# Turning queries and keys in square blocks and through a DRAM scratch, in a two-layer hybrid decoder

## The chip, the cores and the metric

The kernel runs on one core of a Trainium2 chip, in one launch. The metric is the device time of that launch in microseconds. Engines are named as in the profile: PE is TensorE, DVE VectorE, ACT ScalarE, POOL GpSimd, and SP the engine from whose queue nearly all DMAs are issued. L12 is line 12 of the kernel before.

## The reference

The program is a decoder trunk of two layers over 256 tokens with a width of 2048, all in fp32, each sub-layer adding into one residual stream:

```
for i in range(2):
    h = rms_norm(x, mix_norm_g[i])
    mix = fox_attention(h, ...) if i == 0 else dilated_attention(h, ...)
    x = x + mix
    h = rms_norm(x, mlp_norm_g[i])
    x = x + relu(h @ w_up)**2 @ w_down          # 2048 -> 8192 -> 2048
```

`fox_attention` is causal softmax attention of 16 heads of 128 with a bias that grows with a forget gate:

```
q, k, v, f = split(h @ w_in)
q, k = rms_norm(q per head, q_gain), rms_norm(k per head, k_gain)
c = cumsum(log_sigmoid(f + b_f))
p = softmax(causal(q @ k.T * 128**-0.5 + c_query - c_key));  out = (p @ v) @ w_out
```

`dilated_attention` has 8 value heads of width 256. For each of them there are three groups of queries and keys (128 wide, normed per head like those above), with dilations 1, 4 and 16, a causal window of 128 strided steps and a distance bias; the three groups are merged by their softmax denominators.

What matters here: every query and key head is normed over its 128 columns, multiplied by a gain per column, and has to stand with its 128 columns on the partitions before a score can be computed.

## The kernel before

**Products.** Everything large is a product of 256 tokens with 512 columns of a weight matrix, summed over 16 chunks of 128 rows (`product`, L311). An fp32 operand is cut into a rounded part and a remainder (hi and lo), and a chunk is computed by three matmuls for each of the two token tiles (L322 to L324): six matmuls per chunk. The two accumulators of a product take two of the four PSUM buffers of `ps_acc`.

**Weights.** Two chunks come in one load of 512 KB (`load`, L272, on SP's queue, five buffers; for the queries and keys of the dilated layer two DMAs of 256 KB, since a product takes 256 columns of queries and 256 of keys). `split` (L281) casts them on ScalarE (L293) and subtracts on VectorE (L294) into one of five split buffers. When a product has used a split buffer, it calls `split` for the next.

**Jobs.** All other work is written as generators (`Jobs`, L41). A product calls `jobs.tick()` after each chunk, and a job that yields a number goes on so many ticks later; one that yields a key goes on once this key is done. So the code says beside which chunk a step is written. A scheduler then orders the instructions of each engine; each engine runs its own in order.

**Queries and keys.** `qk_chain` (L445) starts at the end of each product of queries and keys: 8 in the first layer, `("fq", j)` and `("fk", j)` for the quarters j = 0 to 3, and 12 in the second, `("dqk", q4, g)` for quarter q4 and group g. It works on two tiles (t = 0, 1) of 128 tokens x 4 heads x 128 columns. ScalarE squares the accumulators into `sq` (L451), VectorE sums them, GpSimd takes the power -0.5 (L458), and three ticks later VectorE writes the normed `qn` (L464). Four ticks after that TensorE transposes the four heads of tile 0 into one PSUM buffer (L472), and a tick later those of tile 1. From PSUM ScalarE writes `whole`, the plain fp32 copy scaled by the gain (L478, for t = 0 alone), and `hi` (L486), and VectorE writes `lo` (L487). Keys need hi and lo for both tiles, queries for tile 1 alone. `sq` and `qn` live in the five buffers of tag "w".

**Heads.** `fox_head` (L631) waits for its quarter's queries and keys, for the gate and the mask, and then 2 * hh + 2 ticks, before its scores are written: a bias matmul (L639), one plain fp32 matmul for tile 0 (L546), and three matmuls with hi and lo for tile 1 (L549). `dil_head` (L681) waits for its three groups and then 4 * i + 2 ticks; the scores of its three groups are one tick apart. While the heads of a quarter are worked on, TensorE goes on with the next products.

Of the kernel before, what the change touches and what calls it, by code (L numbers as in the profile page):

```python
# [9 lines left out]
F32 = mybir.dt.float32  # L10
F32R = mybir.dt.float32r
I32 = mybir.dt.int32  # L12
AF = mybir.ActivationFunctionType
ALU = mybir.AluOpType
# [3 lines left out]
P = 128  # L18
D = 2048
S = 256  # L20
NT = S // P
# [66 lines left out]
def trunk(ctx: ExitStack, tc, x, fox_w_in, fox_b_f, fox_q_gain, fox_k_gain, fox_w_out, dil_w_in,  # L88
          dil_q_gain, dil_k_gain, dil_w_out, mix_norm_g, mlp_norm_g, mlp_w_up, mlp_w_down, out):
    nc = tc.nc  # L90
    jobs = Jobs()
# [3 lines left out]
    wpool = ctx.enter_context(tc.tile_pool(name="wpool", bufs=1))  # L95
    work = ctx.enter_context(tc.tile_pool(name="work", bufs=1))
    small = ctx.enter_context(tc.tile_pool(name="small", bufs=8))
    ps_acc = ctx.enter_context(tc.tile_pool(name="ps_acc", bufs=4, space=PSUM))
    ps_tp = ctx.enter_context(tc.tile_pool(name="ps_tp", bufs=2, space=PSUM))
    ps_sc = ctx.enter_context(tc.tile_pool(name="ps_sc", bufs=2, space=PSUM))  # L100
# [5 lines left out]
    ident = const.tile([P, P], F32, name="ident")  # L106
# [14 lines left out]
    gain = const.tile([P, 4 * KC + 8], F32, name="gain")  # L121
# [111 lines left out]
    for q4 in range(4):  # L233
        for g in range(3):
            c = g * DH * P + q4 * 2 * P
# [67 lines left out]
    def by_column(acc, apart=NC // 2):  # L303
        return acc.rearrange("p (b n h) -> p b h n", n=apart, h=2)

    def halves(t, apart=NC // 2):
        return t.rearrange("p (b h n) -> p b h n", n=apart, h=2)
# [134 lines left out]
        return lambda k: (tag, k // 2)  # L442


    def qk_chain(acc, tag, key, parts):  # L445

        yield (tag, "rstd")
        sq = []
        for t in range(NT):
            s = work.tile([P, NC], F32, tag="w", name=f"sq_{key}_{t}", bufs=5)  # L450
            nc.scalar.activation(halves(s), by_column(acc[t]), AF.Square, scale=rstd[tag][:, t:t + 1])  # L451
            sq.append(s)
        ss = small.tile([P, NT, 4], F32, tag="ss", name=f"ss_{key}")
        for t in range(NT):
            nc.vector.tensor_reduce(ss[:, t, :], sq[t].rearrange("p (h d) -> p h d", h=4), AX.X, ALU.add)
        nc.vector.tensor_scalar(ss, ss, 1.0 / P, EPS, ALU.mult, ALU.add)
        rq = small.tile([P, NT, 4], F32, tag="rq", name=f"rq_{key}")
        nc.gpsimd.tensor_tensor(rq, ss, mhalf.rearrange("p (t h) -> p t h", t=NT), ALU.pow)  # L458
        yield 3
        qn = []  # L460
        for t in range(NT):
            nc.vector.tensor_scalar_mul(rq[:, t, :], rq[:, t, :], rstd[tag][:, t:t + 1])
            q = work.tile([P, 4, P], F32, tag="w", name=f"qn_{key}_{t}", bufs=5)
            nc.vector.tensor_mul(q.rearrange("p (h g) d -> p h g d", h=2),  # L464
                                 acc[t].rearrange("p (g d h) -> p h g d", h=2, g=2),
                                 rq[:, t, :].rearrange("p (h g) -> p h g", h=2).unsqueeze(3).to_broadcast([P, 2, 2, P]))
            qn.append(q)
        yield 4
        for t in range(NT):
            pt = ps_tp.tile([P, 4, P], F32, tag="tp", name=f"ptq_{key}_{t}")  # L470
            for h in range(4):
                nc.tensor.transpose(pt[:, h, :], qn[t][:, h, :], ident)  # L472
            for c, nh, gcol, (whole, hi, lo) in parts:
                src = pt[:, c // P:c // P + nh, :]
                gc = gain[:, gcol:gcol + 1]
                keys = hi.shape[2] == S
                if t == 0:
                    nc.scalar.activation(whole, src, AF.Copy, scale=gc)  # L478
                    if not keys:
                        continue  # L480
                at = slice(t * P, (t + 1) * P) if keys else slice(0, P)
                for i in range(nh):

                    order = [x.rearrange("p (h n) -> p h n", h=2) for x in (hi[:, i, at], lo[:, i, at])]
                    of = src[:, i, :].rearrange("p (n h) -> p h n" if keys else "p (h n) -> p h n", h=2)
                    nc.scalar.activation(order[0], of, AF.Copy, scale=gc)  # L486
                    nc.vector.scalar_tensor_tensor(order[1], of, gc, order[0].bitcast(F32), ALU.mult, ALU.subtract)  # L487
            yield 1
        jobs.done.add(key)

    def v_chain(acc, tag, key, dst):
# [228 lines left out]
    def dilated(tag):  # L720
        for q4 in range(4):
            qTs = [heads_pair(f"dqT{q4}_{g}", g, False) for g in range(3)]
            kTs = [heads_pair(f"dkT{q4}_{g}", 3 + g, True) for g in range(3)]
            for g in range(3):
                product(keys_h(tag), lhs_h(tag),
                        lambda acc: qk_chain(acc, tag, ("dqk", q4, g),
                                             [(0, 2, DIL_G + g, qTs[g]), (2 * P, 2, DIL_G + 3 + g, kTs[g])]))
            vt = values(f"dv{q4}")
            for i in range(2):
                jobs.spawn(dil_head(q4, i, qTs, kTs, vt))  # L730
            product(keys_h(tag), lhs_h(tag), lambda acc: v_chain(acc, tag, ("dv", q4), vt))
# [114 lines left out]
    tag = "n0"  # L846
    for j in range(4):
        sel = make_sel(j)
        qT = [heads_pair(f"fqT{j}_{i}", i, False) for i in range(2)]
        kT = [heads_pair(f"fkT{j}_{i}", 3 + i, True) for i in range(2)]  # L850
        vt = values(f"fv{j}")
        product(keys_h(tag), lhs_h(tag), lambda acc: qk_chain(
            acc, tag, ("fq", j), [(0, 2, FOX_G, qT[0]), (2 * P, 2, FOX_G, qT[1])]))
        if j == 0:
            jobs.need("wf")
            gate(tag)
        product(keys_h(tag), lhs_h(tag), lambda acc: qk_chain(
            acc, tag, ("fk", j), [(0, 2, FOX_G + 1, kT[0]), (2 * P, 2, FOX_G + 1, kT[1])]))

        for hh in range(4):  # L860
            jobs.spawn(fox_head(j, hh, qT, kT, vt, sel))
        product(keys_h(tag), lhs_h(tag), lambda acc: v_chain(acc, tag, ("fv", j), vt))
# [42 lines left out]
```

## Time and profile before

| | |
|---|---|
| time, median of 3 runs | 2186.88 us (2186.87 to 2187.01) |
| profiled execution | 2186.94 us |
| its span, first to last instruction | 2185.1 us |
| granted clock | 1.0 |
| TensorE matmul busy | 2175.9 us (100%) |
| VectorE, ScalarE, GpSimd busy | 1372.8, 1099.9, 49.3 us |
| moved by DMA | 425.78 MB, 195 GB/s |

All busy times and starts come from the one profiled execution. Matmuls are pipelined: the duration shown for one (0.38 us for 512 columns) is longer than the time by which it moves the next, which is read from the starts of neighbours. A line "A <- B: total, times, longest" in the list of waits says that A sat idle until B was done.

### The profile page before, as it was taken

Reading aid. Unit: us, or ns where it says so; the run is one execution under the profiler, and the core shown is the slowest. Engines: PE = TensorE matmul, PEld = TensorE weight load, DVE = VectorE, ACT = ScalarE, POOL = GpSimd, SP = SyncE. Lnnn points to the kernel's source line nnn. Section 1 sums busy time; section 2 is a strip of 40 time slices with the busy share of each in tenths; the row PEclk is TensorE's granted clock in tenths of the full one; section 3 lists DMA queues with packets and bytes.
Section 4 is the critical chain, followed back from the end, with each engine's and each line's share of the span. In section 5 each row is a group of like instructions: output and inputs, shape, how many; then the busy total and the mean of one; then the engine's idle time right before and its main releaser. Section 6 shows DMA issues by size and latency. Waiting matters only on the chain.

```text
span 2185.1 us, 29948 instructions
## 1 busy us (share of the span) xinstructions
PE 2175.9 (100%) x11464; PEld 1937.9 (89%) x11464; DVE 1372.8 (63%) x1810; ACT 1099.9 (50%) x1517; POOL 49.3 (2%) x52
## 2 busy tenths in 40 slices
PE   9999999999999999999999999999999999999999
PEld 7888888998998998998888888888988988988988
DVE  6776685655665565566666767665655655655564
ACT  6565555544454454454555555555544544544442
POOL 1011000000000000000000000000000000000000
PEclk9999999999999999999999999999999999999999
DMA  7566555656666666665555565656656656656664
GB/s 246 171 183 186 175 175 198 196 203 203 201 202 204 202 201 203 202 201 198 195 186 176 182 193 168 198 178 191 201 203 202 201 203 202 201 203 204 201 212 144
DMA packets 248832, 425.78 MB, mean 195 GB/s; under 512 B 16824, under 2 KB 66544, under 8 KB 248688
## 3 DMA queue, kind: packets, MB, share of 16 engines
q1 hardware_dynamic: 248096, 423.19, 60.4%
q8 instruction: 90, 1.47, 0.3%
q10 hardware_dynamic: 560, 0.66, 0.1%
q14 instruction: 54, 0.44, 0.1%
q0 software_dynamic: 32, 0.02, 0.0%
HBM read 421.70 MB, written 2.10 MB: 194 GB/s over the span
## 4 chain that ended last, share of the span: by engine, by line
PE 98%; DVE 1%; ACT 0%; issue 0%; DMA 0%; POOL 0%; ACTq 0%; POOLq 0%
PE acc L322 21%; PE acc L324 21%; PE acc L323 21%; PE up_n3a_acc L370 5%; PE up_n1a_acc L370 5%; PE up_n3a_tp L370 3%; PE up_n3a_sc L370 3%; PE up_n1a_sc L370 3%; PE up_n1a_tp L370 3%; PE up_n1a_acc L374 3%; PE up_n3a_acc L374 3%; PE up_n1a_tp L374 1%; PE up_n1a_sc L374 1%; PE up_n3a_sc L374 1%; PE up_n3a_tp L374 1%; PE ptx_n L406 1%
## 5 line engine op out<-in xcount | busy, mean ns | idle before, releaser
L294 DVE TENSOR_TENSOR wl<-raw,wh 128x1024 fp32r<-128x1024 f32 (+1 forms) x801 | 978.7, 1223 | 703.8 <-ACT wh L293 697.0
L293 ACT CAST wh<-raw 128x1024 fp32r<-128x1024 f32 (+1 forms) x801 | 838.4, 1047 | 881.9 <-PE acc L324 525.8
L322 PE MATMUL acc<-wh,hT_n 128*128 128x512 f32 x896 | 346.0, 387 | 0.2 <-ACT wh L293 0.2
L323 PE MATMUL acc<-wl,hT_n 128*128 128x512 f32 x896 | 340.3, 380 | 0.1
L324 PE MATMUL acc<-wh,hT_n 128*128 128x512 f32 x896 | 340.2, 380 | 0.0
L322 PE MATMUL acc<-wh,aTh_n1a 128*128 128x512 f32 x512 | 194.5, 380 | 0.0
L323 PE MATMUL acc<-wl,aTh_n1a 128*128 128x512 f32 x512 | 194.0, 379 | 0.0
L324 PE MATMUL acc<-wh,aTl_n1a 128*128 128x512 f32 x512 | 194.0, 379 | 0.0
L324 PEld LDWEIGHTS acc<-wh,hT_n 128*128 128x128 f32 x896 | 169.7, 189 | 23.9
L322 PEld LDWEIGHTS acc<-wh,hT_n 128*128 128x128 f32 x896 | 169.6, 190 | 21.9 <-ACT wh L293 0.6
L323 PEld LDWEIGHTS acc<-wl,hT_n 128*128 128x128 f32 x896 | 170.0, 190 | 21.3 <-DVE wl L294 0.4
L322 PE MATMUL acc<-wh,aTh_n3a 128*128 128x512 f32 x480 | 181.9, 379 | 0.0
L323 PE MATMUL acc<-wl,aTh_n3a 128*128 128x512 f32 x480 | 181.9, 379 | 0.0
L324 PE MATMUL acc<-wh,aTl_n3a 128*128 128x512 f32 x480 | 181.9, 379 | 0.0
L370 PE MATMUL up_n3a_acc<-hT_n,wh 128*128 128x512 f32 x512 | 181.6, 382 | 0.0
L370 PE MATMUL up_n1a_acc<-hT_n,wh 128*128 128x512 f32 x512 | 181.6, 382 | 0.0
L374 PE MATMUL up_n1a_acc<-hT_n,wl 128*128 128x256 f32 x512 | 139.6, 273 | 0.0
L374 PE MATMUL up_n3a_acc<-hT_n,wl 128*128 128x256 f32 x512 | 139.6, 273 | 0.0
L324 PEld LDWEIGHTS acc<-wh,aTl_n1a 128*128 128x128 f32 x512 | 96.8, 189 | 13.7
L323 PEld LDWEIGHTS acc<-wl,aTh_n1a 128*128 128x128 f32 x512 | 96.8, 189 | 13.6
L370 PEld LDWEIGHTS up_n1a_acc<-hT_n,wh 128*128 128x128 f32 x512 | 96.8, 189 | 13.5
L322 PEld LDWEIGHTS acc<-wh,aTh_n1a 128*128 128x128 f32 x512 | 96.8, 189 | 13.5
(732 smaller groups left out, 3207.1 us busy)
## 6 DMA issues: line engine op xcount, KB each, us to landing
raw<-in_mlp_w_up_dram SPq DMA_DIRECT2D x256, 512.0 KB, 4.2
raw<-in_mlp_w_down_dram SPq DMA_DIRECT2D x256, 512.0 KB, 3.8
raw<-in_dil_w_in_dram SPq DMA_DIRECT2D x192, 256.0 KB, 2.9
raw<-in_fox_w_in_dram SPq DMA_DIRECT2D x95, 512.0 KB, 3.9
raw<-in_fox_w_out_dram SPq DMA_DIRECT2D x32, 512.0 KB, 3.6
raw<-in_dil_w_in_dram SPq DMA_DIRECT2D x32, 512.0 KB, 3.7
raw<-in_dil_w_out_dram SPq DMA_DIRECT2D x32, 512.0 KB, 3.6
out_dram<-x SPq DMA_DIRECT2D x7, 256.0 KB, 5.9
```

Source lines behind the costliest of these rows:

```text
L293: issued["cast"] = nc.scalar.copy(hi[:, part, :], raw[:, part, :])
L294: nc.vector.tensor_sub(lo[:, part, :], raw[:, part, :], hi[:, part, :].bitcast(F32))
L322: nc.tensor.matmul(acc[t], ah[:, tok], hi, start=first, stop=False)
L323: nc.tensor.matmul(acc[t], ah[:, tok], lo, start=False, stop=False)
L324: issued["product"] = nc.tensor.matmul(acc[t], al[:, tok], hi, start=False, stop=last)
L370: issued["product"] = nc.tensor.matmul(banks[b], hi[:, i, col], in_turn(tokens.rearrange("p x s -> p (x s)"), P // 2), start=first, stop=last)
L374: nc.tensor.matmul(banks[b][:, 0:S], lo[:, i, col], in_turn(tokens[:, 0, :], P // 2), start=False, stop=False)
L406: issued["transposed"] = nc.tensor.transpose(pt[:, i, t * P:(t + 1) * P], xt[n][:, t, c:c + P], ident)
```

## The change

In 18 of the 20 chains, all but `("fk", 3)` and `("dqk", 3, 2)`, the transposition is done in two other ways together. VectorE transposes each 32 x 32 block of `qn` in place of the whole (`nc.vector.transpose`, into the buffer of `sq`). The blocks are then moved to their places by DMAs: for each tile, four stores of 64 KB, one per 32 partitions, from `sq` into a DRAM scratch, and one reload of 256 KB from it into `qn`. All of these are issued from SP's queue. The rest of the chain is written 8 + 1 + 1 ticks after `qn`, where it was 4 + 1 + 1, and reads SBUF instead of PSUM: ScalarE scales two heads at once, into `whole` or, for the second tile, into `sq[0]`, and copies that into `hi`, and VectorE subtracts for `lo`.

```diff
+    dram = ctx.enter_context(tc.tile_pool(name="dram", bufs=1, space=bass.MemoryType.DRAM))
...
+    by_engine = {("fk", 3), ("dqk", 3, 2)}
+
     def qk_chain(acc, tag, key, parts):
...
             qn.append(q)
-        yield 4
-        for t in range(NT):
-            pt = ps_tp.tile([P, 4, P], F32, tag="tp", name=f"ptq_{key}_{t}")
-            for h in range(4):
-                nc.tensor.transpose(pt[:, h, :], qn[t][:, h, :], ident)
-            for c, nh, gcol, (whole, hi, lo) in parts:
...
+        if key in by_engine:
+            yield 4
...
+            jobs.done.add(key)
+            return
+
+
+        for t in range(NT):
+            turned = sq[t].rearrange("p (j h r) -> p j h r", j=4, h=4)
+            nc.vector.transpose(turned.rearrange("p j h r -> p h j r"),
+                                qn[t].rearrange("p h (j c) -> p h j c", c=32))
+            blocks = dram.tile([4, 32, 4, P], F32, tag="blocks", name=f"blocks_{key}_{t}", bufs=4)
+            for i in range(4):
+                nc.sync.dma_start(blocks[:, :, i, :].rearrange("j c x -> c j x"), sq[t][32 * i:32 * i + 32].rearrange("p (j x) -> p j x", j=4))
+            nc.sync.dma_start(qn[t], blocks.rearrange("j c i x -> (j c) (i x)").rearrange("p (h d) -> p h d", h=4))
+        yield 8
+        for t in range(NT):
+            yield 1
+            for n, (c, nh, gcol, (whole, hi, lo)) in enumerate(parts):
                 keys = hi.shape[2] == S
...
+                src = qn[t].rearrange("p i (h r) -> p h i r", h=4)[:, c // P:c // P + nh]
+                to = sq[0].rearrange("p (n i x) -> p n i x", n=2, i=2)[:, n] if t else whole
+                nc.scalar.activation(to.rearrange("p h (i r) -> p h i r", i=4), src, AF.Copy, scale=gain[:, gcol:gcol + 1])
+                if t == 0 and not keys:
+                    continue
                 at = slice(t * P, (t + 1) * P) if keys else slice(0, P)
...
+                a, b = (x[:, :, at].rearrange("p i (h n) -> p i h n", h=2) for x in (hi, lo))
+                of = to.rearrange("p i (n h) -> p i h n" if keys else "p i (h n) -> p i h n", h=2)
+                nc.scalar.copy(a, of)
+                nc.vector.tensor_sub(b, of, a.bitcast(F32))
         jobs.done.add(key)
```

More of the change, by code (lines that the diff above doesn't have):

```diff
@@ L467, in qk_chain @@
             qn.append(q)
-        yield 4
-        for t in range(NT):
-            pt = ps_tp.tile([P, 4, P], F32, tag="tp", name=f"ptq_{key}_{t}")
-            for h in range(4):
-                nc.tensor.transpose(pt[:, h, :], qn[t][:, h, :], ident)
-            for c, nh, gcol, (whole, hi, lo) in parts:
-                src = pt[:, c // P:c // P + nh, :]
-                gc = gain[:, gcol:gcol + 1]
-                keys = hi.shape[2] == S
[L477 to L480, printed above, removed]
-                at = slice(t * P, (t + 1) * P) if keys else slice(0, P)
[L482 to L488, printed above, removed]
+        if key in by_engine:
+            yield 4
+            for t in range(NT):
+                pt = ps_tp.tile([P, 4, P], F32, tag="tp", name=f"ptq_{key}_{t}")
+                for h in range(4):
+                    nc.tensor.transpose(pt[:, h, :], qn[t][:, h, :], ident)
+                for c, nh, gcol, (whole, hi, lo) in parts:
+                    src = pt[:, c // P:c // P + nh, :]
+                    gc = gain[:, gcol:gcol + 1]
+                    keys = hi.shape[2] == S
+                    if t == 0:
+                        nc.scalar.activation(whole, src, AF.Copy, scale=gc)
+                        if not keys:
+                            continue
+                    at = slice(t * P, (t + 1) * P) if keys else slice(0, P)
+                    for i in range(nh):
+                        order = [x.rearrange("p (h n) -> p h n", h=2) for x in (hi[:, i, at], lo[:, i, at])]
+                        of = src[:, i, :].rearrange("p (n h) -> p h n" if keys else "p (h n) -> p h n", h=2)
+                        nc.scalar.activation(order[0], of, AF.Copy, scale=gc)
+                        nc.vector.scalar_tensor_tensor(order[1], of, gc, order[0].bitcast(F32), ALU.mult, ALU.subtract)
+                yield 1
+            jobs.done.add(key)
+            return
@@ new lines, in qk_chain @@
+        yield 8
+        for t in range(NT):
+            yield 1
+            for n, (c, nh, gcol, (whole, hi, lo)) in enumerate(parts):
+                keys = hi.shape[2] == S
+                src = qn[t].rearrange("p i (h r) -> p h i r", h=4)[:, c // P:c // P + nh]
+                to = sq[0].rearrange("p (n i x) -> p n i x", n=2, i=2)[:, n] if t else whole
+                nc.scalar.activation(to.rearrange("p h (i r) -> p h i r", i=4), src, AF.Copy, scale=gain[:, gcol:gcol + 1])
+                if t == 0 and not keys:
+                    continue
+                at = slice(t * P, (t + 1) * P) if keys else slice(0, P)
+                a, b = (x[:, :, at].rearrange("p i (h n) -> p i h n", h=2) for x in (hi, lo))
+                of = to.rearrange("p i (n h) -> p i h n" if keys else "p i (h n) -> p i h n", h=2)
+                nc.scalar.copy(a, of)
+                nc.vector.tensor_sub(b, of, a.bitcast(F32))
```

## The prediction

> **What bounds the kernel now.** I read the page first (span, busy times, the chain that ended last), then who waited for whom, then TensorE's timeline around one product of queries and keys.
>
> ```profile
> span 2185.1 us, 29948 instructions
> ...
> PE 2175.9 (100%) x11464; PEld 1937.9 (89%) x11464; DVE 1372.8 (63%) x1810; ACT 1099.9 (50%) x1517; POOL 49.3 (2%) x52
> ...
> PEclk9999999999999999999999999999999999999999
> ...
> q1 hardware_dynamic: 248096, 423.19, 60.4%
> ...
> PE 98%; DVE 1%; ACT 0%; issue 0%; DMA 0%; POOL 0%; ACTq 0%; POOLq 0%
> ```
>
> 98% of the chain lies on TensorE, at the full granted clock. A busy PE need not be a PE at its peak, so the waits decide. TensorE's own list is this short:
>
> ```profile
> PE spare L116 <- POOL ident masks.py:199: 2.5, 1, 2.5
> PE ps_g_mix L135 <- DMA g_mix<-in_mix_norm_g_dram: 1.9, 1, 1.9
> PE sc_d L546 <- DVE sd L693: 0.8, 4, 0.2
> PE pc L610 <- DVE g_lf L607: 0.2, 1, 0.2
> PE acc L322 <- ACT wh L293: 0.2, 1, 0.2
> ```
>
> After the start it waits 1.2 us in all. Everybody else waits for TensorE:
>
> ```profile
> DVE wl L294 <- ACT wh L293: 697.0, 592, 1.8
> ACT wh L293 <- PE acc L324: 525.8, 375, 2.0
> ...
> ACT wh L293 <- DMA raw<-in_fox_w_in_dram: 4.6, 5, 3.1
> ```
>
> ```profile
> SPq L272 <- DVE wl L294: 1310.3, 620, 4.4
> ```
>
> ScalarE's weight casts wait until TensorE releases a split buffer, VectorE's subtractions wait for the casts, and SP's loads wait for the subtractions; the reverse, a cast waiting for its load, happened five times. So an instruction taken from TensorE is worth the time by which it moves the next product, as long as nothing new makes TensorE wait.
>
> **What is removed: 144 transposes.** Of 20 chains, 18 lose 2 tiles x 4 transposes: 36 groups of four. Their price is read from the starts of the products around them (second key product, the timeline of PE):
>
> ```profile
> 139.83 0.38 PE L322 MATMUL acc<-wh,hT_n 128*128 128x512 f32 x1
> ...
> 141.55 0.38 PE L324 MATMUL acc<-wh,hT_n 128*128 128x512 f32 x1
> 141.77 0.60 PE L472 MATMUL ptq_('fk', 1)_0_1504<-ident,qn_('fk', 1)_0_1463 128*128 128x128 f32 x4
> 142.13 0.46 PE L322 MATMUL acc<-wh,hT_n 128*128 128x512 f32 x1
> 142.43 0.38 PE L323 MATMUL acc<-wl,hT_n 128*128 128x512 f32 x1
> ...
> 147.83 0.33 PE L639 MATMUL sc_f<-negc,sel 128*128 128x384 f32 x1
> 147.99 0.38 PE L546 MATMUL sc_f<-fkT_0w,fqT_0w 128*128 128x128 f32 x2
> 148.13 0.36 PE L549 MATMUL sc_f<-fkT_0h,fqT_0h 128*128 128x256 f32 x1
> 148.32 0.28 PE L549 MATMUL sc_f<-fkT_0l,fqT_0h 128*128 128x256 f32 x1
> ```
>
> From 139.83 to 141.55 lie eight steps, so a product advances TensorE by 0.215 us, and a step of the jobs (six products) by 1.29 us. From the L324 at 141.55 to the L323 at 142.43 pass 0.88 us where two steps would be 0.43: a group costs 0.45 us. 36 x 0.45 = 16.2 us. Nothing on TensorE takes their place.
>
> The Trainium skill ("TensorE: Matmul & The Clock Gate", Part 4: PE-mode transpose) gives about 275 ns for one transpose inside a kernel. By that figure as a cost, 144 of them would be worth an estimated 39.6 us. The starts above do not bear it out as a cost: 0.45 us per four is 0.11 us each.
>
> **What is added on VectorE and ScalarE.** The written order of the changed kernel has both block transposes right behind the second qn. No row shows such a transpose. The bounds are other 128x512 operations: 0.42 us (the cast to sel) and 0.74 us (a subtraction from PSUM, L496); I take 0.68, the qn product.
>
> ```profile
> 140.04 0.68 DVE L464 TENSOR_TENSOR qn_('fk', 1)_1_1466<-acc,rq_('fk', 1)_1434 128x512 f32<-128x512 f32 x1
> 140.64 2.35 DVE L294 TENSOR_TENSOR wl<-raw,wh 128x1024 fp32r<-128x1024 f32 x2
> ...
> 157.65 0.74 DVE L496 SCALAR_TENSOR_TENSOR fv1l<-acc,rstd_n,fv1h 128x512 fp32r<-128x512 f32 x1
> ...
> 159.44 0.42 DVE L677 CAST sel<-self 128x512 fp32r<-128x512 f32 x1
> ```
>
> Two per chain, 36 in all: 24 us of VectorE, which is idle 37% of the span; the following weight subtraction comes 1.4 us later. The subtractions and copies behind the transposition become fewer and wider, about as much work as before. Priced at nothing: the cover is that a weight split is made four buffers ahead of its use, 4 x 2 x 1.29 = 10.3 us.
>
> ```profile
> 135.54 1.05 ACT L293 CAST wh<-raw 128x1024 fp32r<-128x1024 f32 x1 [0.95 <-ACT sq_('fk', 1)_1_1428 L451]
> 138.13 1.05 ACT L293 CAST wh<-raw 128x1024 fp32r<-128x1024 f32 x1 [1.53 <-PE acc L324]
> ...
> 142.41 0.47 ACT L478 ACTIVATE fkT_0w<-ptq_('fk', 1)_0_1504,gain 128x256 f32<-128x256 f32 x1 [0.68 <-PE ptq_('fk', 1)_0_1504 L472]
> ```
>
> ```profile
> L515 DVE TENSOR_TENSOR oTfl<-po_f,oTfh 128x256 fp32r<-128x256 f32 x16 | 6.6, 416 | 0.0
> ```
>
> Casts come every 2.59 us and end 1.05 us later, the subtraction some 1.2 us after that (half of 2.35 above): about 8 us of the 10.3 remain.
>
> **What is added on SP: ten DMAs per chain, and waits in its queue.** Eight stores of 64 KB, two reloads of 256 KB. The order on SP is: four stores of the first tile, three of the second, reload 0 (waits until the four have landed), the eighth store, two weight loads, reload 1 (waits for its four stores). The weight loads behind them wait with them.
>
> ```profile
> raw<-in_dil_w_in_dram SPq DMA_DIRECT2D x192, 256.0 KB, 2.9
> ...
> out_dram<-x SPq DMA_DIRECT2D x7, 256.0 KB, 5.9
> ...
> out_dram<-x ACTq DMA_DIRECT2D x1, 128.0 KB, 1.9
> ```
>
> ```profile
> L765 SPq DMA_DIRECT2D out_dram<-x x6: 356/357/366, 2119.6 to 2161.7; - x6
> ```
>
> The next line is that of L272, the weight loads, between 130 and 152 us:
>
> ```profile
> DMA to landing us min/median/max: 3.9/4.5/5.5
> ```
>
> An issue takes 0.36 us. A store lands after 1.9 us at best (128 KB, nothing beside it) and 5.9 at worst (256 KB beside loads); I take 1.9, since 64 KB is nearer to the first, and keep the other for a rival. A reload lands after 2.9 (256 KB) to 4.5 us (the 512 KB loads in this window).
>
> On the second key product: qn ends at 140.72, the transposes at 141.4 and 142.1; the fourth store leaves at 142.5 and lands at 144.4; reload 0 goes out then, the eighth store at 144.8, landing at 146.7; reload 1 goes out then and lands between 149.6 and 151.2. SP is held some 5.7 us, two loads in between. Its cover: a load is issued when its buffer is free, five weight steps (12.9 us) ahead of its cast; less 2.3 for cast and subtraction and 5.5 for the slowest landing, 5.1 us remain, and then the 8 us above. Queue share: 0.5 MB written and 0.5 MB read per chain and 20.7 us (16 job steps), 18 MB on 423, beside a queue at 60.4%: priced at nothing.
>
> **Who waits for the result.** The chain now ends 8 + 1 + 1 steps after qn instead of 4 + 1 + 1, so the scores of its heads stand four steps later. 147.83 was step 11; without the two groups step 15 is 141.77 + 8 x 1.29 = 152.1. The written order puts three more products behind the first score, so L549, which needs both tiles, comes at 153.05 and the one with fkT_0l at 153.45. ScalarE reaches the second tile's scaling only after the seventh weight cast behind the squares, which TensorE's pace allows at 135.54 + 6 x 2.59 = 151.1; so it starts at 152.1, and reload 1 (151.2 at the latest by the rows) is there. A scaling takes 0.47 (L478 above), a copy of 128x256 takes
>
> ```profile
> L514 ACT CAST oTfh<-po_f 128x256 fp32r<-128x256 f32 x16 | 5.9, 368 | 6.4 <-PE po_f L513 6.4
> ```
>
> 0.37, the subtraction 0.42 (L515). Two scalings and a copy make fkT_0h ready at 153.4, and the subtraction fkT_0l at 153.85: 0.4 us late. I take 0.5. This is met at the first head of the first three quarters of the forgetting attention: 1.5 us. In the dilated layer the scores of the last group come two steps (2.6 us) later, so the first three quarters there wait for nothing by these rows; I add 1.5 us for landings that vary. The later heads, and the two products left on TensorE, wait as before.
>
> **The sum.** The profiled execution took 2186.94 us, 1.84 more than its span, and agrees with the median of 2186.88. 2186.94 - 16.2 + 3 = 2173.7, so 2174. With no stall it is 2170.7.
>
> **Rivals.**
> Half eaten: the four stores of a tile (256 KB) together land like the 256 KB store, 5.9 us after the first: reload 0 at 147.3, the eighth store, alone, issued at 147.7, lands at 149.6 (after 1.9) to 151.6 (after 3.9, half way to 5.9), reload 1 at 152.5 to 156.1. ScalarE then waits 0.4 to 4.0 us. With the 0.5 us from above, three forgetting heads at up to 4.5 and three dilated at up to 1.9 make up to 19 us, in the middle some 10: 2186.94 - 16.2 + 10 = 2181. For it: that row stands beside weight loads, as these stores will. Against it: these are a quarter of its size.
>
> Slower: every store lands like that row. Reload 0 goes out at 148.4, the eighth store lands at 154.7, reload 1 at 159.2, 7.1 us after ScalarE wants it: 7.6 x 3 + 5.0 x 3 = 38 us, less 16.2 is +22: 2209. It decides from 4.7 us per forgetting head (3 x 4.7 + 3 x 2.1 = 20.4), a round trip some 5 us above mine. SP's hold would then pass 13 us and use up the loads' cover too.
> The Trainium skill ("DMA: Bandwidth & Descriptors", Rules for kernel authors) speaks for this side: it warns against transposing by a plain DMA with a rearranged access pattern, 19 times slower than the hardware's. No run here shows such a DMA, and this one moves runs of 512 bytes, the elements inside the blocks being turned by VectorE.
>
> More than the sum: each transpose is worth its whole shown duration (0.27 us): 2186.94 - 39 = 2148. The starts above speak against it. That the change does less than it says is excluded by the order: 144 transposes are gone from TensorE's.
>
> **How the numbers follow.** Forecast, 2170 to 2179: 0.71. Half eaten, 2179 to 2188: 0.15, half of it below 2182.5. Slower: 0.12. More gain: 0.02. What can be told from no change is 0.2%, 4.4 us. So faster 0.80 (0.71 + 0.07 + 0.02), same 0.08, slower 0.12. The range 2170 to 2184 holds the forecast and over half of the second case.
>
> **What would show it.** Right: TensorE's busy time some 16 us lower, ordinary 0.215 us steps where the groups stood, a total of a few us of PE waits at L549 or its counterpart in three to six places, block transposes near 0.7 us, stores landing in about 2 us and ScalarE's scaling of the second tile hardly waiting for its DMA. Wrong: stores landing in 4 us or more, PE waits of 3 us and more at the first scores of each quarter, or weight casts waiting for raw loads around the chains.

## The result and the profile after

| | before | after |
|---|---|---|
| time, median | 2186.88 us (2186.06 to 2187.01, 6 runs) | 2201.18 us (2196.70 to 2209.25, 6 runs) |
| profiled execution | 2186.94 us | 2206.46 us |
| its span | 2185.1 us | 2204.7 us |
| mean granted clock | 1.0 | 0.995 |

The changed kernel is slower: ratio 1.0073, 95% interval 1.0061 to 1.0084. The forecast was 2174, within 2170 to 2184. The kernel before repeats within 1 us, the changed one within 12.6, and its shortest run (2196.70 us) has the highest mean clock (0.998), its longest (2209.25 us) the lowest (0.994). The page of the changed kernel (lines of the changed file: L323 to L325 are the products, L579 and L582 the scores):

```profile
span 2204.7 us, 29840 instructions
PE 2171.6 (98%) x11320; PEld 1932.2 (88%) x11320; DVE 1382.7 (63%) x1793; ACT 1101.0 (50%) x1500; POOL 48.5 (2%) x52
PE 81%; DMA 7%; DVE 4%; issue 3%; SPq 2%; ACT 2%; POOL 1%; ACTq 0%; DVEq 0%; POOLq 0%
```

The 144 transposes are gone, but TensorE's busy time fell by only 4.3 us (2175.9 to 2171.6) where 16.2 were forecast, and its idle time, span less busy, rose from 9.2 to 33.1 us. The chain that ended last lies on TensorE for 81%, where it was 98%. Who TensorE waits for, in the changed kernel (total, times, longest):

```profile
PE sc_d L579 <- DVE sd L726: 10.8, 5, 4.1
PE sc_f L582 <- ACT fkT_0h L520: 10.2, 3, 3.9
PE tq_('dqk', 3, 2)_0_12793 L477 <- DVE qn_('dqk', 3, 2)_0_12752 L468: 2.8, 1, 2.8
```

Nearly all of this lies at the first heads of the first three quarters of both layers; the last line is one of the two chains whose transposes stayed on TensorE. On the second key product, the timeline of TensorE:

```profile
155.19 0.33 PE L672 MATMUL sc_f<-negc,sel 128*128 128x384 f32 x1
...
156.01 0.38 PE L325 MATMUL acc<-wh,hT_n 128*128 128x512 f32 x1
160.29 0.58 PE L582 MATMUL sc_f<-fkT_0h,fqT_0h 128*128 128x256 f32 x1 [3.90 <-ACT fkT_0h L520]
...
161.51 0.63 PE L324 MATMUL acc<-wl,hT_n 128*128 128x512 f32 x1
161.94 0.63 PE L325 MATMUL acc<-wh,hT_n 128*128 128x512 f32 x1
...
163.18 0.38 PE L325 MATMUL acc<-wh,hT_n 128*128 128x512 f32 x1
163.40 0.38 PE L323 MATMUL acc<-wh,hT_n 128*128 128x512 f32 x1
```

The score comes 3.9 us late, and then, until 163.18, a product advances TensorE by 0.43 us instead of 0.215. By 10 us windows (the length, then TensorE's, weight loads', VectorE's, ScalarE's and GpSimd's busy time, the granted clock, the share of the DMA engines, and GB/s):

```profile
150.00:160.00 10.00, 6.39 (x31) 5.30 (x29) 5.28 (x6) 4.73 (x9) 0.00 (x0) 0.99 0.85 269
160.00:170.00 10.00, 9.71 (x47) 8.67 (x48) 8.33 (x23) 6.21 (x17) 0.00 (x0) 0.84 0.54 177
```

Before, the clock was 1.00 in both windows. So a late score is paid twice: by its wait, and by a lower clock behind it. ScalarE's timeline shows where the wait comes from:

```profile
131.27 0.51 ACT L513 ACTIVATE fqT_0w<-qn_('fq', 1)_0_1283,gain 128x256 f32<-128x256 f32 x1 [2.03 <-DMA qn_('fq', 1)_0_1283<-blocks_('fq', 1)_0_1289]
...
136.51 0.91 ACT L513 ACTIVATE sq_('fq', 1)_0_1246<-qn_('fq', 1)_1_1286,gain 128x256 f32<-128x256 f32 x2 [1.12 <-DMA qn_('fq', 1)_1_1286<-blocks_('fq', 1)_1_1296]
...
137.92 0.68 ACT L455 ACTIVATE sq_('fk', 1)_0_1430<-acc,rstd_n 128x512 f32<-128x512 f32 x1
...
148.92 1.05 ACT L294 CAST wh<-raw 128x1024 fp32r<-128x1024 f32 x1 [1.54 <-PE acc L325]
153.46 0.51 ACT L513 ACTIVATE fkT_0w<-qn_('fk', 1)_0_1467,gain 128x256 f32<-128x256 f32 x1 [3.49 <-DMA qn_('fk', 1)_0_1467<-blocks_('fk', 1)_0_1473]
...
159.02 0.91 ACT L513 ACTIVATE sq_('fk', 1)_0_1430<-qn_('fk', 1)_1_1470,gain 128x256 f32<-128x256 f32 x2 [0.89 <-DMA qn_('fk', 1)_1_1470<-blocks_('fk', 1)_1_1480]
159.84 0.40 ACT L520 CAST fkT_0h<-sq_('fk', 1)_0_1430 128x256 fp32r<-128x256 f32 x1
```

ScalarE runs in order. It waits for a reload at 131.27, 136.51, 153.46 and 159.02, and everything behind these scalings waits too: weight casts and, at 137.92, the squares of the next chain. SP's queue and the block transposes between them:

```profile
145.58 0.68 DVE L468 TENSOR_TENSOR qn_('fk', 1)_1_1470<-acc,rq_('fk', 1)_1438 128x512 f32<-128x512 f32 x1
146.18 0.70 DVE L500 STREAM_TRANSPOSE sq_('fk', 1)_0_1430<-qn_('fk', 1)_0_1467 128x512 f32<-128x512 f32 x1
146.81 0.67 DVE L500 STREAM_TRANSPOSE sq_('fk', 1)_1_1432<-qn_('fk', 1)_1_1470 128x512 f32<-128x512 f32 x1
```

```profile
146.91 1.79 SPq L504 DMA_DIRECT2D blocks_('fk', 1)_0_1473<-sq_('fk', 1)_0_1430  x4
148.80 1.37 SPq L504 DMA_DIRECT2D blocks_('fk', 1)_1_1480<-sq_('fk', 1)_1_1432  x3
150.47 0.34 SPq L505 DMA_DIRECT2D qn_('fk', 1)_0_1467<-blocks_('fk', 1)_0_1473  x1
150.86 0.43 SPq L504 DMA_DIRECT2D blocks_('fk', 1)_1_1480<-sq_('fk', 1)_1_1432  x1
151.34 0.97 SPq L273 DMA_DIRECT2D raw<-in_fox_w_in_dram  x2
153.72 0.34 SPq L505 DMA_DIRECT2D qn_('fk', 1)_1_1470<-blocks_('fk', 1)_1_1480  x1
```

The order is the one forecast. The first block transpose ends at 146.88, reload 1 goes out at 153.72 and has landed at 159.02, 12.1 us after the transpose. Over the whole kernel, ScalarE's waits for reloads add up to 65.2 us in its list of waits. Over all chains, the issues of the stores (first line) and of the reloads (second):

```profile
DMA to landing us min/median/max: 1.7/2.1/3.8
```

```profile
DMA to landing us min/median/max: 2.7/4.6/6.0
```

In the dilated layer the wait takes one more turn. VectorE, then ScalarE, then TensorE:

```profile
1251.07 0.43 DVE L521 TENSOR_TENSOR dqT_2l<-sq_('dqk', 1, 2)_0_10980,dqT_2h 128x256 fp32r<-128x256 f32 x1 [1.01 <-ACT dqT_2h L520]
1251.42 0.42 DVE L521 TENSOR_TENSOR dkT_2l<-sq_('dqk', 1, 2)_0_10980,dkT_2h 128x256 fp32r<-128x256 f32 x1
1251.75 0.55 DVE L726 SCALAR_TENSOR_TENSOR sd<-dist,sc_d 128x384 f32<-128x384 f32 x1
```

```profile
1249.84 0.91 ACT L513 ACTIVATE sq_('dqk', 1, 2)_0_10980<-qn_('dqk', 1, 2)_1_11023,gain 128x256 f32<-128x256 f32 x2 [1.03 <-DMA qn_('dqk', 1, 2)_1_11023<-ks_('dqk', 1, 2)_1_11033]
```

```profile
1252.44 0.77 PE L579 MATMUL sc_d<-dkT_2w,dqT_2w 128*128 128x128 f32 x2 [4.14 <-DVE sd L726]
```

The third score of the head needs one of the two PSUM buffers that the first two hold. The bias step that frees it (L726) stands in VectorE's queue behind the subtractions of the last group, which wait for ScalarE's copies and so for the reload.

### The profile page after: what moved, and what is told of

Same layout as the page of the kernel before. It is cut to its first block, busy times and chain, and to the rows that moved or that the text cites. A ratio compares the mean times of both kernels' runs of the same rounds, so it can differ in the third digit from the quotient of the medians.

```text
span 2204.7 us, 29840 instructions
## 1 busy us (share of the span) xinstructions
PE 2171.6 (98%) x11320; PEld 1932.2 (88%) x11320; DVE 1382.7 (63%) x1793; ACT 1101.0 (50%) x1500; POOL 48.5 (2%) x52
## 4 chain that ended last, share of the span: by engine, by line
PE 81%; DMA 7%; DVE 4%; issue 3%; SPq 2%; ACT 2%; POOL 1%; ACTq 0%; DVEq 0%; POOLq 0%
PE acc L323 16%; PE acc L324 16%; PE acc L325 16%; PE up_n3a_acc L371 5%; PE up_n1a_acc L371 5%; PE up_n3a_sc L371 3%; PE up_n3a_tp L371 3%; PE up_n1a_sc L371 3%; PE up_n1a_tp L371 3%; PE up_n1a_acc L375 3%; PE up_n3a_acc L375 3%; DVE wl L295 2%; DMA raw<-in_dil_w_in_dram 2%; SPq L504 1%; PE up_n1a_tp L375 1%
## 5 line engine op out<-in xcount | busy, mean ns | idle before, releaser
L323 PE MATMUL acc<-wh,hT_n 128*128 128x512 f32 x896 | 347.0, 388 | 0.0
L325 PE MATMUL acc<-wh,hT_n 128*128 128x512 f32 x896 | 342.7, 383 | 0.0
L323 PE MATMUL acc<-wh,aTh_n1a 128*128 128x512 f32 x512 | 194.5, 380 | 0.0
L325 PE MATMUL acc<-wh,aTl_n1a 128*128 128x512 f32 x512 | 194.0, 379 | 0.0
L325 PEld LDWEIGHTS acc<-wh,hT_n 128*128 128x128 f32 x896 | 171.4, 191 | 24.8
L323 PEld LDWEIGHTS acc<-wh,hT_n 128*128 128x128 f32 x896 | 171.8, 192 | 22.9 <-ACT hT_n L412 0.3
L323 PE MATMUL acc<-wh,aTh_n3a 128*128 128x512 f32 x480 | 181.9, 379 | 0.0
L325 PE MATMUL acc<-wh,aTl_n3a 128*128 128x512 f32 x480 | 181.9, 379 | 0.0
L325 PEld LDWEIGHTS acc<-wh,aTl_n1a 128*128 128x128 f32 x512 | 96.8, 189 | 13.7
L323 PEld LDWEIGHTS acc<-wh,aTh_n1a 128*128 128x128 f32 x512 | 96.8, 189 | 13.5
```

Source lines behind the costliest of these rows:

```text
L323: nc.tensor.matmul(acc[t], ah[:, tok], hi, start=first, stop=False)
L325: issued["product"] = nc.tensor.matmul(acc[t], al[:, tok], hi, start=False, stop=last)
```

## The experiments

Theory A, formed from these rows: the loss is the wait for the reloads, spread by the in-order queues of ScalarE and VectorE, and the clock behind each wait. Rival B: the held SP queue and the traffic delay the weights.

**What the transposes are worth: double_transposes.** The kernel before, each group of four done twice.

```diff
-            for h in range(4):
-                nc.tensor.transpose(pt[:, h, :], qn[t][:, h, :], ident)
+            for _ in range(2):
+                for h in range(4):
+                    nc.tensor.transpose(pt[:, h, :], qn[t][:, h, :], ident)
```

> The kernel before, with each group of four transposes on TensorE done twice into the same place: 40 groups more. By the price read from the starts of the products (0.45 us a group) 2186.9 + 18 = 2205 us (2203 to 2207). If transposes are hidden (theory C): 2187 to 2189. If each cost its shown duration of 0.27 us: 2230.

2204.73 us, ratio 1.0083 (1.0066 to 1.0099): 17.85 us over the 2186.88 of before for 40 groups, 0.446 each. The first term of the sum holds.

**The change without its round trip: no_round_trip.** The stores and reloads are left out, so the scores are computed from blocks that stay where VectorE left them.

```diff
...
-            for i in range(4):
-                nc.sync.dma_start(blocks[:, :, i, :]..., sq[t][32 * i:32 * i + 32]...)
-            nc.sync.dma_start(qn[t], blocks...)
...
-                src = qn[t]...
-                to = sq[0]...
+                src = sq[t]...
+                to = qn[0]...
```

> The stores and reloads are left out: VectorE transposes the blocks, and the blocks are then read where they lie, so the scores are computed from queries and keys whose blocks were not moved. All other instructions and the later steps stay. A and B alike: 2186.9 - 16.2 = 2170 to 2173 us, no waits at the scores, full clock. C, or VectorE's block transposes as the cause: 2187 or more.

2172.02 us (2171.79 to 2172.28), ratio 0.9933 (0.9918 to 0.9948).

```profile
PE 2159.6 (100%) x11320; PEld 1924.7 (89%) x11320; DVE 1384.4 (64%) x1793; ACT 1103.1 (51%) x1500; POOL 48.7 (2%) x52
```

TensorE's busy time is 16.3 us below that of before, and the block transposes, the wider copies and the later heads cost it next to nothing. So the round trips cost the changed kernel 2201.2 - 2172.0 = 29 us. In the profiled execution (2204.7 - 2170.1 = 34.6 us of span) 12.0 us of that are TensorE busy for longer with the same matmuls, and 22.6 are idle.

**The round trip made, but not waited for: unread_round_trip and unread_apart.** Both issue every DMA, and compute the scores from the unmoved blocks. First with both reloads into `qn[1]`, then with every DMA's buffers as in the change:

```diff
-            nc.sync.dma_start(qn[t], blocks...)
+            nc.sync.dma_start(qn[1], blocks...)     # unread_round_trip alone
...
-                src = qn[t]...
+                src = sq[t]...                      # both; to = qn[0] in the first
```

> The changed kernel with all its stores and reloads still issued at their places, both reloads of a chain into qn[1], which nobody reads: as in no_round_trip the scalings read the blocks where VectorE left them, so the scores are of unmoved blocks. Traffic and SP's queue are then those of the changed kernel; only the wait for the result is gone. Theory A (the loss is the wait for the reload, through ScalarE's in-order queue, and the clock behind it): 2172 to 2176, within 0.2% of no_round_trip's 2172.0. Rival B (the held SP queue and 18 MB of traffic delay the weights, and that costs TensorE time by itself): 2180 to 2200; each us above 2172 is B's share of the changed kernel's 29.

2185.38 us, ratio 0.9995 (0.9986 to 1.0005), which looks like 13 us for B. But the first reload overwrites what the second block transpose still has to read:

```profile
DVE sq_('fk', 1)_1_1432 L500 <- DMA qn_('fk', 1)_1_1470<-blocks_('fk', 1)_0_1473: 4.5, 1, 4.5
```

VectorE waited there as ScalarE does in the change, so this kernel separates nothing.

> As unread_round_trip, but every store and reload keeps the buffer it has in the changed kernel; only the scalings read the blocks in sq[t] in place of qn[t]. In unread_round_trip the first reload went into qn[1], which VectorE's second block transpose still had to read, so VectorE waited 4 to 4.5 us for a reload in several chains, and its 2185.4 is no measure of traffic alone. Here nobody waits for a reload except whoever takes its buffer next. Theory A (the loss is the wait for the result, with ScalarE's queue and the clock behind it): 2172 to 2176. Rival B (held SP queue and traffic): 2180 to 2190; each us above 2172.0 is B's share of the changed kernel's 29.

2174.49 us (2172.02 to 2175.45), ratio 0.9942 (0.9927 to 0.9956). All stores and reloads are issued and land. The held queue and the traffic do delay the weights (ScalarE waits 25.9 us in all for loads, against 5.5 in no_round_trip), but TensorE hardly notices: they cost about 2.5 us, the wait for the result and what follows from it about 27.

**Later scores: late_scores.** The heads of the first three quarters four ticks (5.2 us) later.

```diff
-        yield 2 * hh + 2
+        yield 2 * hh + 2 + (4 if j < 3 else 0)
...
-        yield 4 * i + 2
+        yield 4 * i + 2 + (4 if q4 < 3 else 0)
```

> The chains and their DMAs stay as in the changed kernel; the heads of the first three quarters of each attention layer write their scores four job steps (5.2 us) later. Theory A (the loss is TensorE waiting at the first scores of a quarter for the second reload, and the lower clock behind these waits): the waits of 3 to 4 us are covered, the 16 us of the transposes are left as gain, 2169 to 2176 us. Theory B (the DMAs of the round trip hold up the weight loads all along): the time hardly changes, 2195 to 2205. Theory C (the transposes on TensorE cost nothing, so there was nothing to gain): not below 2187.

2189.0 us (2183.73 to 2194.56), ratio 1.0009 (0.9999 to 1.0018). 12 us come back: more than B expected, and less than A in this first form, in which the waits at the first scores were the whole loss. The forgetting layer's scores no longer wait for `fkT_0h`, but ScalarE is still held (57.3 us of waits for reloads) and others are late (`sc_d` 6.7 us, `ptp_f` 3.3). More time ahead of the score alone is no remedy.

**Fewer chains by DMA: early_chains and urgent_chains.** The chains whose scores come first stay on TensorE (24 groups of four go), or they alone go by DMA (12 groups go).

```diff
-    by_engine = {("fk", 3), ("dqk", 3, 2)}
+    by_engine = {("fk", j) for j in range(4)} | {("dqk", j, 2) for j in range(4)}     # early_chains
+    by_engine = {("fq", j) for j in range(4)} | {("dqk", j, g) for j in range(4) for g in range(2)} | {("fk", 3), ("dqk", 3, 2)}     # urgent_chains
```

> Only the 12 chains whose result is needed a product or more later (the queries of the first layer, groups 0 and 1 of the second) go through blocks and DMAs; all keys of the first layer and group 2 of the second stay on TensorE. A: 24 groups of four transposes at 0.45 us are 10.8 us of gain and nobody waits at the scores: 2175 to 2180 us. B: 12 of the 18 round trips, so about two thirds of the loss stay, 2193 to 2200. C: not below 2187.

2186.45 us (2182.74 to 2188.63), ratio 0.9998 (0.9989 to 1.0008): 9 us above the 2177.4 that it would be without loss (2172.0 of no_round_trip and 12 groups more on TensorE, 5.4), which neither theory had expected. No product of the remaining 12 chains is wanted soon, yet TensorE waits, for the next chain's `qn`:

```profile
PE tq_('dqk', 3, 2)_0_12799 L477 <- DVE qn_('dqk', 3, 2)_0_12758 L468: 1.9, 1, 1.9
...
PE tq_('dqk', 2, 2)_0_11933 L477 <- DVE qn_('dqk', 2, 2)_0_11892 L468: 1.5, 1, 1.5
```

By these rows it is ScalarE's queue at work (42.1 us of waits for reloads): a chain with time to spare holds ScalarE and so delays one that has none. early_later, below, puts this to the test.

> The opposite of early_chains: only the six chains that the next scores wait for (keys of quarters 0 to 2, group 2 of quarters 0 to 2) go through blocks and DMAs. Gain 12 groups x 0.45 = 5.4 us. A with the waits as they were: 2187 - 5.4 + 30 = 2211. A2 (part of each wait comes from the chain before, whose round trip held ScalarE): the waits are about 2.5 us shorter each, 2188 to 2198 us. B: one third of the traffic, 2185 to 2192.

2196.77 us, ratio 1.0043 (1.0028 to 1.0058). Without loss it would be 2182.8 (2172.0 and 24 groups more), so six chains by themselves lose 14 us. With the 9 us that the other twelve lose by themselves this makes 23 of the 29; neither by itself accounts for the rest. Their forgetting scores wait 6.3 us in all against 10.2 in the change, which fits A: here no query chain holds ScalarE ahead of the key chain's squares, and what is left is the chain's own round trip.

**ScalarE's queue left free: later_scalings.** Three more ticks between `qn` and the scalings (the heads follow three ticks later too), and the scalings placed behind the weight cast written last.

```diff
-        yield 8
+        yield 11
...
+                with behind(issued["cast"]):
                     nc.scalar.activation(to..., src, AF.Copy, scale=gain[:, gcol:gcol + 1])
```

> As the changed kernel, but the steps behind the round trip are written 11 + 1 + 1 job steps after qn, not 8 + 1 + 1, and each scaling is kept behind the newest weight cast on ScalarE, so that two more casts (5.2 us) stand before the first scaling; the heads follow three steps later. Theory A2 (what is left of the loss once the scores are late is ScalarE's queue: it waits in order for a reload, and the weight casts and the next chain's squares behind it come late): ScalarE hardly waits for a DMA, 2172 to 2178 us. Theory A alone (only the waits at the first scores): as late_scores, about 2187. Theory B (the DMAs beside the weight loads): 2185 or more.

2182.8 us (2179.78 to 2187.72), ratio 0.9984 (0.9975 to 0.9993): 18 of the 29 us come back with every DMA as before, less than A2 expected. ScalarE's waits for reloads fall to 6.0 us. How much of the 18 is the freed queue and how much the later heads, these runs do not tell apart; late_scores, with heads four ticks later and ScalarE still held, gave 12. On the second key product ScalarE, and TensorE's wait behind it:

```profile
153.17 1.04 ACT L294 CAST wh<-raw 128x1024 fp32r<-128x1024 f32 x1 [2.59 <-DMA raw<-in_fox_w_in_dram]
154.12 0.50 ACT L514 ACTIVATE fkT_0w<-qn_('fk', 1)_0_1467,gain 128x256 f32<-128x256 f32 x1
```

```profile
158.55 0.38 PE L583 MATMUL sc_f<-fkT_0h,fqT_0h 128*128 128x256 f32 x1 [0.91 <-ACT fkT_0h L521]
```

ScalarE no longer waits for the reload, but for a weight load; such waits add up to 34.9 us here, against 12.7 in the change. From 153.17 it is busy without a gap until it casts `fkT_0h` at 158.08, and TensorE waits 0.91 us for that cast. So here some of what is left of the loss came by way of a late weight load.

**Two ways around SP's queue: reload_first and pool_queue.** Loads written after a chain are issued behind its latest reload; or stores and reloads are issued by GpSimd.

```diff
-                with hold(t[:, 0, 0:1]):
+                with hold(t[:, 0, 0:1]), behind(*([issued["reload"]] if "reload" in issued else [])):
...
-            nc.sync.dma_start(qn[t], blocks...)
+            issued["reload"] = nc.sync.dma_start(qn[t], blocks...)     # reload_first
...
-                nc.sync.dma_start(...)
+                nc.gpsimd.dma_start(...)                               # pool_queue, all ten
```

> As the changed kernel, but a weight load written after a reload is also issued after it, so the second reload no longer stands behind two weight loads on SP and in the DMA queues. A and A2: the second reload lands some 2 us earlier and each of the waits at the first scores shrinks by about as much: 2186 to 2194 us. B: the weight loads now wait longer, so 2201 or more.

2306.41 us, ratio 1.0547 (1.0531 to 1.0563), far from every expectation.

```profile
144.83 1.65 SPq L273 DMA_DIRECT2D raw<-in_fox_w_in_dram  x2
159.00 1.79 SPq L504 DMA_DIRECT2D blocks_('fk', 1)_0_1473<-sq_('fk', 1)_0_1430  x4
```

The edit held back not two loads but every load written after a chain: nothing left SP for 12.5 us, the weights ran out (TensorE waits 26.0 us for casts), and with them the squares came late. It says nothing on A or B, and shows what it costs to stop the loads behind a chain.

> As the changed kernel, with the stores and reloads issued from GpSimd's queue, so that SP issues weight loads alone and never waits for a store. B in the form that SP is held: the loss goes, 2171 to 2180 us. A and A2: the round trip is as long or longer, 2195 to 2210 us, with the same waits at the first scores.

2287.73 us, ratio 1.0463 (1.0445 to 1.048), outside both expectations.

```profile
157.36 2.22 POOL L504 DMA_DIRECT2D blocks_('fk', 1)_0_1473<-sq_('fk', 1)_0_1430  x4 [1.28 <-DVE sq_('fk', 1)_0_1430 L500]
...
164.32 0.57 POOL L505 DMA_DIRECT2D qn_('fk', 1)_0_1467<-blocks_('fk', 1)_0_1473  x1 [3.12 <-DMA blocks_('fk', 1)_0_1473<-sq_('fk', 1)_0_1430]
...
169.62 0.56 POOL L505 DMA_DIRECT2D qn_('fk', 1)_1_1470<-blocks_('fk', 1)_1_1480  x1 [4.18 <-DMA blocks_('fk', 1)_1_1480<-sq_('fk', 1)_1_1432]
```

SP is free, and the kernel is 87 us slower than with SP held: reload 1 goes out 12.3 us after the first store began, against 6.8 on SP, since the stores landed after 4.2 us in the median instead of 2.1. The page counts these DMAs under another kind of queue (software_dynamic, 18.90 MB) than SP's (hardware_dynamic). On this product ScalarE then waits 12.4 us for reload 0. So a free SP does not bring the loss back, and a longer round trip makes it larger; GpSimd, which now waits for the stores, also has a step of every chain in its queue, and what that adds was not measured.

**The clock by itself: early_transposes.** The kernel before, without any DMA more: in the six chains whose scores come first, `qn` and TensorE's transposes are written earlier, the heads where they were.

```diff
+        early = key in [("fk", 0), ("fk", 1), ("fk", 2), ("dqk", 0, 2), ("dqk", 1, 2), ("dqk", 2, 2)]
-        yield 3
+        yield 0 if early else 3
...
-        yield 4
+        yield 0 if early else 4
...
+        if early:
+            yield 7
         jobs.done.add(key)
```

> The kernel before, with no DMA added: in six chains (keys of the first three quarters, last group of the first three dilated quarters) qn and TensorE's transposes are written 3 + 4 ticks earlier, and the heads stay where they were, so that TensorE waits for qn six times, by an estimate from the rows of before 2 to 4 us each. Theory A with the clock (behind a wait of about 4 us TensorE runs at a lower granted clock for some us): the time rises by about 1.5 times the sum of the new waits, as in the changed kernel (23.9 us more idle, 12.0 us more busy than without round trips), and the profile shows slices of lower clock behind the waits. Rival (a wait costs its own length): the time rises by the sum of the waits, busy time stays at 2175.9.

2202.68 us (2202.27 to 2206.01), ratio 1.0072 (1.0055 to 1.0088). Profiled: 2206.0 us. TensorE waits for `qn` six times, 1.9 to 2.6 us, 12.8 in all; its busy time rises by 6.5 us (2175.9 to 2182.4), which the rival, a wait that costs its own length, does not allow. On the second key product:

```profile
139.50 0.38 PE L322 MATMUL acc<-wh,hT_n 128*128 128x512 f32 x1
142.05 1.06 PE L473 MATMUL ptq_('fk', 1)_0_1442<-ident,qn_('fk', 1)_0_1437 128*128 128x128 f32 x4 [2.17 <-DVE qn_('fk', 1)_0_1437 L465]
...
144.62 0.63 PE L322 MATMUL acc<-wh,hT_n 128*128 128x512 f32 x1
145.04 0.61 PE L323 MATMUL acc<-wl,hT_n 128*128 128x512 f32 x1
...
145.71 0.38 PE L322 MATMUL acc<-wh,hT_n 128*128 128x512 f32 x1
145.92 0.38 PE L323 MATMUL acc<-wl,hT_n 128*128 128x512 f32 x1
```

After a wait of 2.2 us TensorE advances by 0.42 us per product for some 3.5 us. The total rose by 1.5 times the waits in this execution, the slowest of four (19.1 over 12.8), and by 15.8 us in the median, which would be 1.2 times if the waits were the same there. So a wait can bring the clock down without any added DMA. It doesn't always: three of the six waits (1.9, 2.2 and 2.2 us) went with a 10 us window at a clock of 0.83 to 0.86, and the longest, 2.6 us, with none. The traces do not show what decides. (The 23.9 us in the expectation are idle time over the kernel before; over no_round_trip it is 22.6.)

**Together: early_later and later_both.** later_scalings with the chains of early_chains; later_scalings with the first three quarters' heads two ticks later.

> later_scalings and early_chains together: the four key chains of the forgetting layer and the last group of the dilated layer's four quarters go by TensorE (8 chains), the other 12 by blocks, with scalings three ticks later and behind the latest cast. 24 groups of four are gone, so 2186.9 - 24 x 0.45 = 2176.1 without any loss. Theory A (what early_chains lost, 9 us, was ScalarE's queue held by reloads, which delayed the next chain's squares and so its TensorE transposes): those waits are gone, 2176 to 2179.5. Rival B (the loss is traffic and the held queue): 2182 to 2187, as early_chains.

2177.96 us (2177.39 to 2180.13), ratio 0.9963 (0.995 to 0.9976), the fastest that leaves no work out: 9 us less than before, 23 less than the change, 0.6 above the loss-free 2177.4 of its 12 chains. ScalarE waits for no reload any more; it waits 21.6 us for weight loads, and TensorE shows next to nothing of that. The longest waits that the chains leave:

```profile
PE sc_d L580 <- DVE sd L727: 0.8, 4, 0.2
PE tq_('dqk', 3, 2)_0_12799 L477 <- DVE qn_('dqk', 3, 2)_0_12758 L468: 0.8, 1, 0.8
```

> later_scalings with the heads of the first three quarters of both layers two ticks later (2.6 us); 18 chains by blocks. No-stall time 2171 to 2172. In later_scalings the scores of these heads still waited 7.4 us, at most 1.9 at once. Theory A (the rest of the loss is scores that come before their keys): 2172 to 2177. Rival B (the rest is weight loads late behind the held SP queue): 2180 to 2184, unchanged. Rival C (later heads wait for something else, as when they were moved by four): over 2184.

2179.79 us (2177.81 to 2181.46), ratio 0.9968 (0.9955 to 0.9981), between the expectations: the scores' waits are nearly gone, others (3.4 us at `po_f`) have come, and some 8 us above no_round_trip remain. Of these the queue and the traffic explain 2.5 by unread_apart; the rest stays unassigned.

## Why the prediction was wrong

**Right.** A group of four transposes at 0.45 us, 16.2 us for 36: 0.446 by double_transposes, and the busy time of no_round_trip fell by 16.3. The loss-free 2170.7: 2172.0. Block transposes at 0.68: 0.67 to 0.70. Stores landing after 1.9: 2.1 in the median. The order on SP. SP's hold and the traffic priced at nothing: 2.5 us. Also the places of the waits in the forgetting layer.

**The step that failed: who waits for the result.** In the sum it is the term of 3 us for waits, against 22.6 us of idle time, with nothing beside it for the clock, against 12.0 us of slower matmuls (profiled execution, against no_round_trip). The prediction had the score of the second key product wait 0.5 us for its keys; it waited 3.9. Two terms made that.

First, the chain was taken to start where it started before. That would put `qn`'s end (140.72) 12.3 us ahead of the demand (153.05). In the changed kernel it ended at 146.26, and the demand, one product after 156.01, was at 156.2: 9.9 us. The missing 2.4 us are ScalarE's: it stood idle for 1.1 us until 136.51, waiting for the query chain's reload, and then had that chain's scaling and copies to do until 137.92, with the squares of the key chain behind them. I had asked what is queued behind SP's waiting instructions, and not what is queued behind ScalarE's.

Second, reload 1 was to land 8.2 to 9.8 us after the first block transpose; it took 12.1. It went out after 6.8 us instead of 5.3. Issues of 0.43 us instead of 0.36 make 0.3 of that; the rest is the landing of the stores, which took 2.2 to 2.9 us on this product instead of 1.9. It then landed after 5.3 instead of 2.9 to 4.5, where reload 0 had taken 2.9. Two weight loads of 512 KB stand between the two reloads, and in that window the DMAs moved 269 GB/s, against 157 before; that this is the cause is not shown by itself. 2.4 and 2.3, less the 0.9 us that ScalarE was to have in hand (151.2 to 152.1), make 3.8 on top of the 0.5, so 4.3, against 3.9 measured.

**The dilated layer** was to wait for nothing in its first three quarters by the rows, and got 1.5 us for landings that vary. It waited 10.8 us, through ScalarE's queue, VectorE's queue and the two PSUM buffers of the scores.

**The missing term: the clock.** Every wait was priced at its length. In the profiled execution the loss against no_round_trip is 22.6 us of idle time and 12.0 us of slower matmuls; early_transposes, which adds waits and no DMA, shows slower matmuls behind waits. The Trainium skill ("TensorE: Matmul & The Clock Gate", Part 1: The HAM clock gate) describes this: after an idle window of about 3.4 us the clock is halved, and comes back after as long a busy one. The halving agrees with the trace (0.43 against 0.215 us per product). The threshold does not: in early_transposes waits of 1.9 to 2.2 us were enough at three places.

**The rivals.** "Slower" came true in its sign and nearly in its number (2209 against 2201), and partly by its mechanism: the scores of the first heads waited for reload 1. Its price was wrong, as the stores landed in 2.1 us and not in 5.9. Its chance, 0.12, went by that price alone; the queue and the clock lead to the same end with stores nearly as fast as forecast. The rule of the Trainium skill quoted beside it there ("DMA: Bandwidth & Descriptors", Rules for kernel authors) pointed the right way; that transposes by plain DMA are 19 times slower is shown by no run here, where the length of the round trip cost, and hardly its rate. "Half eaten" had the length of the round trip right (11.1 to 14.7 us from the first block transpose by its figures, 12.1 measured), though by other landings, and the idle time at up to 19 us, against 22.6; it lacked the clock and took the middle of its range.

## What to carry to other kernels

When an instruction on an in-order engine gets a new thing to wait for, list what is queued behind it on that same engine, up to the next iteration of the same chain: a latency that its own consumer can afford is passed on to a chain that can't. In a kernel whose TensorE never waited, price a wait of 2 to 4 us at more than its length: here the clock behind such waits added a half in the two profiled executions, and by the median of early_transposes, if its waits were the same there, nearer a quarter. And take a round trip's length from rows taken where it will run, with its issues and the loads between them, not from the fastest row of its kind.

## What the runs showed of the hardware

A wait of TensorE of 2.2 us can be followed by some 3.5 us in which matmuls advance at half their pace (early_transposes: 0.42 us per product instead of 0.215). The same ten DMAs took nearly twice as long from GpSimd's queue as from SP's until the second reload went out (12.3 against 6.8 us), and an issue occupied GpSimd for about 0.55 us, against 0.43 for most stores and 0.34 for a reload on SP.
